# Attention's head pairs traced with the second head first, in scores and in value blocks

## The chip, the core and the metric

The kernel runs on one core of one Trainium2 chip. The metric is the device time of one execution in microseconds (us). Its engines are TensorE (PE; its weight loads are listed as PEld), VectorE (DVE), ScalarE (ACT), GpSimd (POOL) and SyncE (SP).

## What is computed

Four transformer layers over 512 tokens of width 1024, all in float32: two of a first kind, then two of a second. Every layer is a mixer and a feed-forward network, each between two RMS norms. Half of each mixer is an attention of 8 heads of 64 columns; this is the part that the change touches.

```python
# first kind: dilated windows; the three branches are merged by their log-denominators
for window, dilation in ((128, 1), (512, 4), (2048, 16)):
    o, lse = dilated_branch(q, k, v, window, dilation)
attn = sum(softmax(lses)[..., None] * outs)          # the other half: a gated delta rule
# second kind: every query attends to the keys that an indexer's top-k selects
logits = einsum('bqhd,bsd->bqhs', iq, ik) * 64 ** -0.5
score = einsum('bqh,bqhs->bqs', iw, relu(logits))
top_val, top_idx = top_k(where(allowed, score, -inf), 128)
p = softmax(where(valid, einsum('bqhd,bqkhd->bqhk', q, k[top_idx]) * 64 ** -0.5, -inf))
out = einsum('bqhk,bqkhd->bqhd', p, v[top_idx])      # the other half: pooled means
```

## The kernel before

Tokens lie in four tiles of 128. A dense product is three TensorE matmuls on rounded parts (`mm3`, L289 to L291, two high-by-low terms beside the high-by-high one), with weights split by ACT (L267) and DVE (L269, or POOL).

Attention (`attention`) works on units (i, h): query tile i, head h, 32 units a layer, in order of i. It never gathers keys: scores over the first (i + 1) * 128 keys are masked. Two heads that follow each other form a pair, e = 0 and e = 1. The two share the array: a head's 64 columns of q and k lie in rows 0 to 63 (e = 0) or 64 to 127 (e = 1), and its result lies in the same half of the accumulator. A unit goes through these steps:

- scores on PE into a PSUM buffer: one float32 matmul in the first kind (L783 in `plain_scores`), three rounded ones in the second (L794 in `split_scores`, which the second kind's indexer calls too);
- mask and row minimum on DVE (L827), exponent and row sum on ACT (L829), reciprocal of a pair's sums on DVE (L837), scaling on ACT (L838). In the pair DVE and ACT take e = 0 first;
- transposes on PE, i + 1 of them (L845), into a PSUM buffer; a copy back to SBUF (`tb`, two buffers), by ACT for e = 0 (L851) and by DVE for e = 1 (L849), so that e = 1 is the one whose copy is made last;
- products with the values on PE (`pv2`, L864): for each key block j one matmul of e = 0 and one of e = 1, into the two halves of one accumulator `ax`.

The rows of a unit lie in `xc` (first kind) or `qs` (second kind) for e = 0, and in `ta` for e = 1. Scores and transposes share four PSUM buffers named `mm`. The pair's products are traced some five units behind its scores. In the program listing a float32 matmul is one row; in the trace it is two instructions, so that a pair of blocks is x2 in the listing and x4 in the trace.

Attention runs beside other work that generators weave in: dense products at first, then what is left of the delta rule (L1381, first kind) or of the indexer's top-k (`select`, L1686 and L1687 on DVE, sixteen rounds a tile) and of the pooled half (L1718 to L1740, second kind). The queues' orders aren't written by hand. When the program is built, a scheduler keeps a clock of its own and gives each engine, of what it then holds ready, what was traced first. On the chip each engine takes its instructions in that order and waits for semaphores.

Of the kernel before, what the change touches and what calls it, by code (L numbers as in the profile page):

```python
# [91 lines left out]
class Net:  # L92
# [683 lines left out]
    def plain_scores(self, qT, kT):  # L776


        def scores(ss, i, pr):
            w = (i + 1) * P  # L780
            for e, s in enumerate(ss):
                r = self.head_rows(e)
                self.nc.tensor.matmul(s[:, :w], qT[r, pr, i * P:(i + 1) * P], kT[r, pr, :w], start=True, stop=True)  # L783
        return scores

    def split_scores(self, Q, K):


        def scores(ss, i, pr):
            w, c, k = max(2, i + 1) * P, slice(i * P, (i + 1) * P), K(pr)  # L790
            for n, (a, b) in enumerate(((0, 0), (0, 1), (1, 0))):
                for e, s in enumerate(ss):
                    r = self.head_rows(e)
                    self.nc.tensor.matmul(s[:, :w], Q[a][r, pr, c], k[b][r, :w], start=n == 0, stop=n == 2)  # L794
        return scores
# [8 lines left out]
    def attention(self, pool, scores, v, nmask, k0, first, n_first, buf, free, masked=lambda i: True):  # L804

        nc, V, T = self.nc, self.nc.vector, self.nc.tensor
        units = [(i, h) for i in range(NT) for h in range(8)]
        st, acc, sums, late = {}, {}, {}, []  # L810
        depth = 5
        pair = lambda n: n - n % 2

        def qk2(n):
            i, h = units[n]
            ss = [first() if n < n_first else self.mm() for _ in range(2)]
            scores(ss, i, h // 2)
            sums[n] = self.sm.tile([P, 2], F32, name="asum", bufs=6)
            for e, s in enumerate(ss):
                qk(n + e, s)  # L820

        def qk(n, s):
            i, h = units[n]
            w = (i + 1) * P
            pb = buf(n)
            m = self.sm.tile([P, 1], F32, name="amin", bufs=6)
            V.tensor_tensor_reduce(pb[:, :w], s[:, :w], nmask(i), scale=1.0, scalar=FMAX,  # L827
                                   op0=OP.add, op1=OP.min, accum_out=m)
            nc.scalar.activation(pb[:, :w], pb[:, :w], AF.Exp, bias=m, scale=-1.0,  # L829
                                 accum_out=sums[pair(n)][:, n % 2:n % 2 + 1])  # L830
            st[n] = pb

        def norm(n):

            w, s = (units[n][0] + 1) * P, sums[pair(n)]
            if n % 2 == 0:
                V.reciprocal(s, s)  # L837
            nc.scalar.activation(st[n][:, :w], st[n][:, :w], AF.Copy, scale=s[:, n % 2:n % 2 + 1])  # L838

        def tr(n):  # L840
            i, h = units[n]
            pb = st[n]
            pt = self.mm()
            for j in range(i + 1):
                T.transpose(pt[:, j * P:(j + 1) * P], pb[:, j * P:(j + 1) * P], self.ident)  # L845
            w = (i + 1) * P
            pT = pool.tile([P, S], F32, name="tb", bufs=2)
            if n % 2:
                V.tensor_copy(pT[:, :w], pt[:, :w])  # L849
            else:  # L850
                nc.scalar.activation(pT[:, :w], pt[:, :w], AF.Copy)  # L851
            st[n] = pT

        def pv2(n):


            i, h = units[n]
            pT = [st.pop(n + e) for e in range(2)]
            if h == 0:
                acc[i] = self.ax()  # L860
            o = acc[i]
            for j in range(i + 1):
                for e in range(2):
                    T.matmul(o[self.head_rows(e), h // 2 * P:(h // 2 + 1) * P], v[:, j, (h + e) * 64:(h + e + 1) * 64],  # L864
                             pT[e][:, j * P:(j + 1) * P], start=j == 0, stop=j == i, skip_group_check=True)
            if h == 6:
                late.append((i, acc.pop(i)))

        def out(i, o):
            s = slice(i * P, (i + 1) * P)  # L870
            self.split_out(self.four(o), self.hha[:, k0:k0 + 4, s], self.hla[:, k0:k0 + 4, s])

        for n in range(len(units) + depth + 3):
            if n < len(units) and n % 2 == 0:
                while not masked(units[n][0]):
                    yield
                qk2(n)
            if 0 <= n - 3 < len(units):
                norm(n - 3)
            if late and free():  # L880
                out(*late.pop(0))
            if depth < n <= len(units) + depth and (n - depth) % 2 == 0:
                while late and not free():
                    yield
                if late and units[n - depth - 2][1] == 0:
                    out(*late.pop(0))
                pv2(n - depth - 2)
            if 0 <= n - depth < len(units):
                tr(n - depth)
            yield  # L890
        for i, o in late:
            out(i, o)
# [948 lines left out]
```

## Time and profile before

| | us |
|---|---|
| median of three runs | 2632.26 |
| these runs | 2622.97, 2632.26, 2636.4 |
| the profiled execution | 2618.65 |
| its span, first to last instruction | 2616.9 |
| PE busy | 2573.4 |
| DVE busy | 1645.4 |
| ACT busy | 1205.7 |

PE's busy time counts an instruction from its start to its modelled end, and neighbours overlap; where the distance of two starts is meant, the text says so. "Idle before" is time that an engine stood still ahead of an instruction, with the instruction that released it. Each layer has one stretch in which attention runs with little dense work beside it; in the trace these are 252 to 292 us and 955 to 996 us (first kind) and 1558 to 1613 us and 2154 to 2209 us (second kind).

### The profile page before, as it was taken

To read this page: it belongs to the slowest core of one execution; us is meant where nothing else is said; L and a number is where in the kernel's file an instruction comes from. 1 tells how busy PE (TensorE), PEld (TensorE's weight loads), DVE (VectorE), ACT (ScalarE), POOL (GpSimd) and SP (SyncE) were. 2 spreads that over 40 slices of the span, in tenths; PEclk is the share of its full clock that TensorE was granted. 3 is DMA by queue.
4 is the path that set the end of the run, shared out by engine and by line. 5 is a ranking of instruction groups with operands and counts; after the bars stand their busy time and mean duration, and the time that the engine had idled before them with its cause. 6 is when DMAs were issued, how large, how long until landed. Compare 5 with 4: busy or idle time off the path is not lost. (4 is left out here: it accounts for less than half of the span.)

```text
span 2616.9 us, 37121 instructions
## 1 busy us (share of the span) xinstructions
PE 2573.4 (98%) x14376; PEld 2125.0 (81%) x14376; DVE 1645.4 (63%) x3206; ACT 1205.7 (46%) x2032; POOL 266.5 (10%) x356
## 2 busy tenths in 40 slices
PE   8999999999999999999999999999999999999998
PEld 7877788888888868888888766999888776999887
DVE  6946676664487575666726686776325687776434
ACT  5346543343443464433424456466324556456322
POOL 2100110000120001000002331100002330200000
PEclk9999999999999999999999999999999999999999
DMA  5321213333324112223333222232333221322332
GB/s 161 95 86 52 81 41 97 97 97 91 103 70 121 51 33 81 73 92 94 97 93 93 65 73 64 74 97 89 90 96 94 69 73 52 103 81 89 97 90 95
DMA packets 165817, 221.94 MB, mean 85 GB/s; under 512 B 25760, under 2 KB 112520, under 8 KB 165640
## 3 DMA queue, kind: packets, MB, share of 16 engines
q1 hardware_dynamic: 164247, 216.92, 27.6%
q0 software_dynamic: 832, 2.63, 0.4%
q8 instruction: 113, 1.85, 0.3%
q14 instruction: 65, 0.52, 0.1%
q10 hardware_dynamic: 560, 0.01, 0.0%
HBM read 212.70 MB, written 6.83 MB: 84 GB/s over the span
## 5 line engine op out<-in xcount | busy, mean ns | idle before, releaser
L289 PE MATMUL mm<-hh,wh 128*128 128x512 f32 (+2 forms) x1684 | 633.7, 378 | 3.3 <-ACT wh L267 1.1
L269 DVE TENSOR_TENSOR wl<-wr,wh 128x1024 fp32r<-128x1024 f32 (+1 forms) x286 | 353.7, 1237 | 447.5 <-ACT wh L267 443.8
L290 PE MATMUL mm<-hl,wh 128*128 128x512 f32 (+2 forms) x1684 | 633.2, 376 | 0.0
L291 PE MATMUL mm<-hh,wl 128*128 128x512 f32 (+2 forms) x1684 | 627.1, 374 | 0.0
L267 ACT ACTIVATE wh<-wr 128x1024 fp32r<-128x1024 f32 (+1 forms) x310 | 326.4, 1054 | 587.3 <-PE mm L290 242.3
L289 PEld LDWEIGHTS mm<-hh,wh 128*128 128x128 f32 (+1 forms) x1684 | 317.2, 188 | 68.0 <-ACT wh L267 1.5
L291 PEld LDWEIGHTS mm<-hh,wl 128*128 128x128 f32 (+1 forms) x1684 | 315.6, 188 | 62.3 <-DVE wl L269 0.6
L290 PEld LDWEIGHTS mm<-hl,wh 128*128 128x128 f32 (+1 forms) x1684 | 315.9, 188 | 57.4 <-issue 0.3
L289 PE MATMUL mm<-wh,hh 128*128 128x512 f32 x524 | 213.9, 408 | 0.0
L291 PE MATMUL mm<-wh,hl 128*128 128x512 f32 x524 | 207.8, 397 | 0.0
L290 PE MATMUL mm<-wl,hh 128*128 128x512 f32 x524 | 207.8, 396 | 0.0
L289 PEld LDWEIGHTS mm<-wh,hh 128*128 128x128 f32 x524 | 98.7, 188 | 28.3 <-issue 4.9
L291 PEld LDWEIGHTS mm<-wh,hl 128*128 128x128 f32 x524 | 98.7, 188 | 23.6
L290 PEld LDWEIGHTS mm<-wl,hh 128*128 128x128 f32 x524 | 98.9, 189 | 20.9
L1397 DVE TENSOR_TENSOR hl<-hq,hh 128x512 fp32r<-128x512 f32 x92 | 63.1, 688 | 80.7 <-ACT hh L1396 80.5
L1510 ACT ACTIVATE fy<-fxc,par 128x512 f32<-128x512 f32 x88 | 67.1, 810 | 78.4 <-DVE fxc L1507 78.4
L1396 ACT ACTIVATE hh<-hq 128x512 fp32r<-128x512 f32 x92 | 57.2, 622 | 97.6 <-PE dx L290 78.8
L609 ACT ACTIVATE hh<-x,par 128x256 fp32r<-128x256 f32 x128 | 60.9, 504 | 72.6 <-DVE x L690 72.6
L1507 DVE TENSOR_TENSOR fxc<-mm,rrep 128x512 f32<-128x512 f32 x88 | 60.0, 690 | 29.7 <-PE mm L291 25.4
L864 PE MATMUL ax<-tb,v 128*64 128x128 f32 x640 | 68.9, 286 | 7.8 <-DVE tb L849 7.4
L864 PEld LDWEIGHTS ax<-tb,v 128*64 128x64 f32 x640 | 42.8, 136 | 41.4 <-DVE tb L849 16.9
L269 POOL TENSOR_TENSOR wl<-wr,wh 128x1024 fp32r<-128x1024 f32 x24 | 58.4, 2432 | 111.4 <-ACT wh L267 111.2
(793 smaller groups left out, 5389.8 us busy)
## 6 DMA issues: line engine op xcount, KB each, us to landing
wr<-in_w_ff_dram SPq DMA_DIRECT2D x100, 512.0 KB, 3.7
wr<-in_w_in_dram SPq DMA_DIRECT2D x96, 512.0 KB, 3.7
wr<-in_ffn_w_in_dram SPq DMA_DIRECT2D x176, 256.0 KB, 3.2
wr<-in_ffn_w_out_dram SPq DMA_DIRECT2D x44, 512.0 KB, 3.6
wr<-in_w_out_dram SPq DMA_DIRECT2D x32, 512.0 KB, 3.6
tail<-in_w_ff_dram SPq DMA_DIRECT2D x28, 512.0 KB, 4.4
xt<-in_x_dram SPq DMA_DIRECT2D x4, 512.0 KB, 7.5
scm<-dM SPq DMA_DIRECT2D x2, 1024.0 KB, 4.5
```

The lines of the kernel that those rows point to most:

```text
L267: nc.scalar.activation(h[:, :n], r[:, :n], AF.Copy)
L269: eng.tensor_tensor(lo[:, :n], r[:, :n], h[:, :n].bitcast(F32), op=OP.subtract)
L289: t.matmul(out, ah, bh, start=first, stop=False, skip_group_check=shared)
L290: t.matmul(out, ah, bl, start=False, stop=False, skip_group_check=shared)
L291: t.matmul(out, al, bh, start=False, stop=last, skip_group_check=shared)
L609: nc.scalar.activation(self.hh[k][:, c], self.x[k][:, c], AF.Copy, scale=g)
L864: T.matmul(o[self.head_rows(e), h // 2 * P:(h // 2 + 1) * P], v[:, j, (h + e) * 64:(h + e + 1) * 64], pT[e][:, j * P:(j + 1) * P], start=j ...
L1396: nc.scalar.activation(h, hid[k], AF.Copy)
L1397: V.tensor_tensor(lo, hid[k], h.bitcast(F32), op=OP.subtract)
L1507: V.tensor_tensor(xc[:, 2:], pt, rrep, op=OP.mult)
L1510: nc.scalar.activation(y, xc[:, 2:], AF.Identity, scale=w(2), bias=self.pcol("ffn_conv_b", l, r))
```

## The change

In three loops the second head of a pair is now traced ahead of the first: both kinds of scores, and the products with the values. Nothing else is edited; no tile, wait or instruction is added or taken away.

```diff
         def scores(ss, i, pr):
             w = (i + 1) * P
-            for e, s in enumerate(ss):
+            for e, s in reversed(list(enumerate(ss))):
                 r = self.head_rows(e)
                 self.nc.tensor.matmul(s[:, :w], qT[r, pr, i * P:(i + 1) * P], kT[r, pr, :w], start=True, stop=True)
...
             for n, (a, b) in enumerate(((0, 0), (0, 1), (1, 0))):
-                for e, s in enumerate(ss):
+                for e, s in reversed(list(enumerate(ss))):
                     r = self.head_rows(e)
                     self.nc.tensor.matmul(s[:, :w], Q[a][r, pr, c], k[b][r, :w], start=n == 0, stop=n == 2)
...
             for j in range(i + 1):
-                for e in range(2):
+                for e in (1, 0):
                     T.matmul(o[self.head_rows(e), h // 2 * P:(h // 2 + 1) * P], v[:, j, (h + e) * 64:(h + e + 1) * 64],
                              pT[e][:, j * P:(j + 1) * P], start=j == 0, stop=j == i, skip_group_check=True)
```

What the scheduler makes of it: in the program before, the products of the 64 pairs stand on PE in 100 runs of L864 rows; 36 pairs are split, the first block of e = 0 alone and the rest some instructions later (8 in each layer of the first kind, 10 in each of the second). Now they stand in 64 runs, one for each pair, e = 1 ahead of e = 0. DVE and ACT change the order of some instructions around them, POOL and SP change nothing, so all transfers stand as before.

On PE, in the first layer at tile i = 1 and 2 (the trace's 259.7 to 264.4 us); x1 of L864 is one float32 matmul:

```order
 L783 MATMUL mm<-kT,qT 128x384 x2
-L864 MATMUL ax<-tb,v 64x128 x3
+L864 MATMUL ax<-tb,v 64x128 x4
 L845 MATMUL mm<-cst,ta 128x128 x2
 L845 MATMUL mm<-cst,xc 128x128 x3
-L864 MATMUL ax<-tb,v 64x128
-L783 MATMUL mm<-kT,qT 128x384
-L864 MATMUL ax<-tb,v 64x128 x3
-L783 MATMUL mm<-kT,qT 128x384
+L783 MATMUL mm<-kT,qT 128x384 x2
+L864 MATMUL ax<-tb,v 64x128 x4
```

The single block and the rest of its pair have become one run, and the two scores that stood on either side of that rest stand together ahead of it.

On PE, in the third layer at tile i = 3 (the trace's 1593.7 to 1595.3 us), with the tiles' numbers: mm_14015 holds the scores of e = 0, mm_14016 those of e = 1:

```order
+L794 MATMUL mm_14016<-kT_12618,qT_12620 128x512
+L794 MATMUL mm_14016<-w3_12619,qT_12620 128x512
+L794 MATMUL mm_14016<-kT_12618,w2_12621 128x512
 L794 MATMUL mm_14015<-kT_12618,qT_12620 128x512
 L794 MATMUL mm_14015<-w3_12619,qT_12620 128x512
 L794 MATMUL mm_14015<-kT_12618,w2_12621 128x512
-L794 MATMUL mm_14016<-kT_12618,qT_12620 128x512
-L794 MATMUL mm_14016<-w3_12619,qT_12620 128x512
-L794 MATMUL mm_14016<-kT_12618,w2_12621 128x512
```

Such a pair stays one head after the other; only which head comes first is turned round. In each layer of the second kind five pairs of scores stand so in the changed program, and in each of the first kind two pairs stand with other work between the heads.

On DVE, in the third layer at the same place, before:

```order
L837 RECIPROCAL asum<-asum 128x2
L827 ISA qs,amin<-mm,nm_12617 128x512
L827 ISA amin 128x1
L827 ISA ta,amin<-mm,nm_12617 128x512
L827 ISA amin 128x1
L849 COPY tb<-mm 128x384
L837 RECIPROCAL asum<-asum 128x2
L269 TENSOR_TENSOR wl<-wr,wh 128x1024
```

and now:

```order
L837 RECIPROCAL asum<-asum 128x2
L269 TENSOR_TENSOR wl<-wr,wh 128x1024
L827 ISA qs,amin<-mm,nm_12617 128x512
L827 ISA amin 128x1
L827 ISA ta,amin<-mm,nm_12617 128x512
L827 ISA amin 128x1
L849 COPY tb<-mm 128x384
```

The split of a weight tile for the next product stands ahead of the pair's masks instead of behind the copy; the masks still take `qs` (e = 0) ahead of `ta` (e = 1).

## Rows read from the trace of the kernel before

**Rows 1.** The page: span; engines' busy us (share); a group's busy us, mean ns | idle before.

```profile
span 2616.9 us, 37121 instructions
PE 2573.4 (98%) x14376; PEld 2125.0 (81%) x14376; DVE 1645.4 (63%) x3206; ACT 1205.7 (46%) x2032; POOL 266.5 (10%) x356
...
L269 DVE TENSOR_TENSOR wl<-wr,wh 128x1024 fp32r<-128x1024 f32 (+1 forms) x286 | 353.7, 1237 | 447.5 <-ACT wh L267 443.8
```

**Rows 2.** Timeline of PE, first layer: start, duration, instructions, idle before and its releaser.

```profile
252.68 0.66 PE L864 MATMUL ax<-tb,v 128*64 128x128 f32 x8
...
258.56 0.44 PE L845 MATMUL mm<-cst,ta 128*128 128x128 f32 x2
258.93 0.43 PE L864 MATMUL ax<-tb,v 128*64 128x128 f32 x2
259.29 0.44 PE L845 MATMUL mm<-cst,xc 128*128 128x128 f32 x2
259.66 0.94 PE L783 MATMUL mm<-kT,qT 64*128 64x384 f32 x4
260.53 0.65 PE L864 MATMUL ax<-tb,v 128*64 128x128 f32 x6
261.11 0.44 PE L845 MATMUL mm<-cst,ta 128*128 128x128 f32 x2
261.39 0.49 PE L845 MATMUL mm<-cst,xc 128*128 128x128 f32 x3
...
262.17 0.91 PE L783 MATMUL mm<-kT,qT 64*128 64x384 f32 x2
...
263.59 0.91 PE L783 MATMUL mm<-kT,qT 64*128 64x384 f32 x2
...
283.42 1.09 PE L864 MATMUL ax<-tb,v 128*64 128x128 f32 x14 [0.17 <-DVE tb L849]
...
285.78 1.21 PE L864 MATMUL ax<-tb,v 128*64 128x128 f32 x16
```

**Rows 3.** The same timeline, where PE waits behind a single block.

```profile
256.01 0.91 PE L783 MATMUL mm<-kT,qT 64*128 64x384 f32 x2
257.14 0.91 PE L783 MATMUL mm<-kT,qT 64*128 64x384 f32 x2 [0.21 <-DVE amin L827]
...
270.34 0.55 PE L845 MATMUL mm<-cst,xc 128*128 128x128 f32 x3 [0.31 <-ACT xc L838]
...
274.57 1.73 PE L783 MATMUL mm<-kT,qT 64*128 64x512 f32 x4
```

**Rows 4.** Stretches: us; busy time (instructions) of PE, PEld, DVE, ACT, POOL; granted clock; DMA.

```profile
252.00:294.00 42.00, 41.21 (x278) 25.05 (x277) 32.23 (x108) 32.77 (x72) 0.82 (x2) 1.00 0.05 17
1558.00:1613.00 55.00, 51.33 (x327) 32.15 (x327) 44.90 (x124) 39.20 (x92) 8.79 (x12) 1.00 0.08 22
1575.30:1597.80 22.50, 19.86 (x121) 11.79 (x121) 22.34 (x65) 15.74 (x40) 0.84 (x1) 1.00 0.00 1
```

**Rows 5.** Chain of work that ended last, 1556 to 1592 us, shares by line.

```profile
by line: POOL pu L1722 23.1%; DVE sc L1687 22.7%; DVE m L1686 19.0%; DVE ta L827 5.7%; DVE qs L827 5.7%; DVE tb L849 5.5%; DVE hl L1740 5.5%; DVE pu L1718 3.4%; DVE pu L1732 3.2%; DVE hl L896 1.6%; issue 1.6%; DVE asum L837 1.5%; DVE t L173
```

**Rows 6.** The same chain from 1590 us on: start, time, what.

```profile
1596.86 0.43 PE mm L794
1597.28 0.80 PE ax L864 x10
1598.08 0.68 PE mm L794 x4
...
1599.93 0.36 PE ax L864 x2
...
1611.32 0.36 PE ax L864 x2
```

**Rows 7.** Timeline of DVE, first layer, at a pair of scores with products between.

```profile
279.47 0.69 DVE L827 CUSTOM_DVE_ANT_0 xc<-mm,cst 128x512 f32<-128x512 f32 x1 [0.63 <-PE mm L783]
...
281.32 0.69 DVE L827 CUSTOM_DVE_ANT_0 ta<-mm,cst 128x512 f32<-128x512 f32 x1 [0.47 <-PE mm L783]
```

## The prediction

> **What bounds the kernel now.** I read the page first: PE is busy 98% of the span, no other engine over 63% [rows 1]. So time is saved only where PE does the same work in fewer nanoseconds, and only if nothing else holds PE up there. The granted clock is 1.00, the upper level of 2.4 GHz, in all stretches that the change touches [rows 4], before and after the waits in them, so the clock is not at issue. Next I looked at stretches. In the first layer's attention tail PE is busy 41.2 of 42.0 us, DVE 32.2 and ACT 32.8: PE is nearly full, with some waits. In the third layer's tail PE is busy 51.3 of 55.0 and DVE 44.9; within it, from 1575.3 to 1597.8, DVE is busy 22.34 of 22.50 us [rows 4]. The second and fourth layers repeat the first and third. The chain of waits says the same of the second kind: from 1556 us to 1592 its steps are POOL's and DVE's, the top-k above all (L1686, L1687), and PE has no line in it [rows 5]. From about 1592 on PE comes back into the chain [rows 6]. So a nanosecond saved on PE counts in the first kind's tails and in the last 20 us of the second kind's, and not in the 36 us before these.
>
> **The price of a split pair.** The PE timeline prices it [rows 2]. The single block of e = 0 is x2. It starts at 258.93 and the next instruction starts at 259.29: 0.36 us. The transposes ahead of it start at 258.56, 0.37 before it; where no single stands between, transposes follow transposes after 0.28 (261.11 to 261.39). So a single adds 0.36 + 0.09 = 0.45. What does the pair save when it is whole? The rest without the single (x6) lasts 0.65, a whole pair of two key blocks (x8) 0.66, because the two heads work in different halves of the array at once; with four key blocks the rest (x14) lasts 1.09 and the whole (x16) 1.21. So mending a split saves 0.44 at one or two key blocks, 0.45 - 0.12 = 0.33 at four; for three no whole pair is shown and I take the middle, 0.38, with the other two as its ends.
>
> Splits in a layer of the first kind are 3 with two blocks, 4 with three and 1 with four: 1.32 + 1.52 + 0.33 = 3.2 us. In a layer of the second kind there is 1 with one block, 4 with two, 3 with three and 2 with four: 2.20 + 1.14 + 0.66 = 4.0 us. One pair of scores in each layer of the first kind is mended too: the two heads alone last 0.91 and 0.91, together 0.94 [rows 2], so up to 0.88 more. Over four layers: 2 x (3.2 + 0.9 + 4.0) = 16.2 us of PE time. That is the upper end.
>
> **What of it is given back.** A whole pair starts when e = 1's copy is there. Where PE would wait for that, or for the next thing behind it, the single had filled a gap and its removal buys nothing.
>
> First kind. Three of the eight singles stand ahead of a wait [rows 3]. Behind the one ahead of 256.01 the second score stands still until DVE has freed a buffer (257.14, idle 0.21, and 1.13 us after the first one's start); ahead of 270.34 PE is idle 0.31 for ACT's scaled row; behind the one ahead of 274.57 the two scores last 1.73, since the second waits for its buffer. I take 0.44 + 0.38 + 0.38 = 1.2 off. The mended score needs both buffers at once, and in the same stretch a buffer came late by as much as the wait at 257.14, so I take half of its 0.88. That leaves 3.2 - 1.2 + 0.4 = 2.4 us a layer. Bounds: 0 if every whole pair waits, 4.1 if none does.
>
> Second kind. Six of the ten splits lie between 1556 and 1592 us, where the chain has nothing of PE [rows 5]: one of one block, four of two, one of three, 2.20 + 0.38 = 2.6 us that becomes waiting of PE. Of the four behind, two are steps of the chain, at 1599.93 and 1611.32, each 0.36 long [rows 6]; with three and four blocks they give 0.38 + 0.33 = 0.7. The other two are covered by ACT and DVE. There is one more gain: at 1596.86 one score matmul, then the products (0.80), then the other scores (0.68) stand ahead of DVE's minimum [rows 6], 1.91 us; now the products come last, and the scores run one head after the other. How long this takes is bounded by 0.43 + 0.68 = 1.1 below and 1.9 above (as before); near the upper end, since a head alone loses the overlap: 0.2 us. Sum 0.9 us a layer, bounds 0 and 1.4 + 0.8.
>
> DVE's weight split, moved ahead of a pair's masks, is the same instruction. In the program before, it stood behind the copy; now it delays the masks only if DVE isn't waiting for the scores there, and turning the heads round makes it wait (next part). I cost it at nothing; if that cover is gone it costs its own length, 1.24 us [rows 1], in each of the two layers. Transfers don't move, as SP and POOL have the same instructions in the same order.
>
> Sum: 2 x 2.4 + 2 x 0.9 = 6.6 us. On the profiled execution (2618.65) this gives 2612.0. That execution lies 13.6 below the median, inside the spread of runs (2622.97 to 2636.4) or just under it, so I carry the difference over to the median: 2632.26 - 6.6 = 2625.7 us, a quarter of a per cent.
>
> **The rivals.**
>
> *All of it arrives.* The waits of rows 3 shrink as well, because products and scores that come earlier on PE start DVE and ACT earlier. For: in the first kind DVE itself stands still for scores of PE (0.63 and 0.47 us, [rows 7]), so a faster PE feeds it. Against: 36 us of the second kind's tail hang on DVE and POOL alone. The time: 2632.3 - 16.2 = 2616.1.
>
> *Nothing arrives.* The single of e = 0 was ready work put into time in which PE would have waited for e = 1's copy. Now e = 0 stands behind e = 1 on PE, and if PE waits at each whole pair until the moment at which the rest started before, the 0.65 of the rest becomes the 0.66 of the whole and no more. For: at rows 3's 270.34 PE does stand still for one instruction with others queued behind it. Against: the timeline shows 0.17 to 0.31 us of idle time at such places [rows 2, 3], less than the 0.45 of a single, and none around 258.93. The time: 2632.3, unchanged. The Trainium skill has a rule for this, in "TensorE: Matmul & The Clock Gate", Part 3 on row and column tiling: matmuls start and end in program order, and only weight loads are pulled ahead. By that rule a ready block behind a late one can't pass it, which speaks against the change; the idle 0.31 us at 270.34 agrees. That the order does not change as announced is no separate case: all 36 splits are gone from the listing.
>
> *Slower: scores now end in the wrong order.* DVE still takes e = 0's minimum first, and now e = 0's scores come last. Where both run at once that costs nearly nothing. In pairs that still stand apart (two in each layer of the first kind, five in each of the second), DVE holds a finished e = 1 and waits for e = 0. Price: before, it did e = 0's 0.69 us while PE was at e = 1 [rows 7]; now both follow the later score, so 0.69 us a pair. It decides where DVE has nothing else and its result is waited for at once. In all 14 pairs that would be 9.7 us, 2642; outside the 36 us that hang on DVE anyway it would be two pairs a layer in both kinds, eight in all, 5.5 us, and if the singles give nothing, the time is 2637.8. Against: at 1596.86 the products no longer stand between a pair's scores, so that one ends earlier whichever head is last.
>
> **How the numbers follow.** Chances: the forecast (3 to 10 us faster) 0.60; all of it 0.15; nothing 0.17; slower 0.08. About 0.5%, 13 us, is what a measurement of this kernel can tell from no change. Faster by over that needs nearly the whole 16.2 us: most of the second case and a small part of the first, 0.15. Slower by over 13 us is beyond the worst price above and is left with 0.03, for a wait that I don't see. Within: 0.82. The range goes from 2612 (all of it, and a median some 4 us lucky) to 2639 (the slower case); the runs of before lie 13 us apart, and this more than the change sets its width.
>
> **What would show it right or wrong.** In the profile after: L864 on PE in 64 runs (x4, x8, x12, x16) and no x2 outside the one-block pairs; x12 between the 0.66 of x8 and the 1.21 of x16; transposes of `xc` some 0.28 behind those of `ta`. In the first kind's tails two to three us less from the first whole pair to the dense product behind; waits of PE for DVE's copy at L864 longer than the 0.17 at 283.42 [rows 2]. In the second kind's tails the top-k ends when it did, PE idles more before 1592, and the gain appears behind it. DVE's idle time ahead of L827 at the pairs that stay apart, above the 0.6 of rows 7, would show the slower case. I am wrong if the tails shrink by over 5 us each (waits fall too), if they don't shrink (all was cover), or if time moves in stretches where the listing shows no change.

## The result

In the first comparison the changed kernel took 2612.72 us (median of 7 runs, 2610.84 to 2619.66) beside 2631.78 for the kernel before (7 runs, 2622.97 to 2638.13). The ratio is 0.9944, 95% interval 0.9927 to 0.9962: 0.56% faster, where the forecast was 0.25% (2625.7 us). (This ratio and those below are the comparisons' own estimates and not quotients of the medians; that quotient would be 0.9928 here.) A second comparison, with 12 runs of it and 35 of before, gave 2616.21 beside 2626.18, ratio 0.9969 (0.9956 to 0.9982). So it is faster, by 10 to 19 us of median, and the forecast of 6.6 us was too small. The 19 are in part chance: in four later comparisons the kernel before has medians of 2624.04 to 2626.18, and not 2631.78. Yet the two profiled executions lie 6.85 us apart (2618.65 and 2611.80), almost the forecast. Both facts have to be explained, and the second turned out to be partly luck: in the one profile the clock did not fall in the second kind's tails, in the other it did.

### The profile page after: what moved, and what is told of

It reads as the page before. It is cut to its first block, busy times and chain, and to the rows that moved or that the text cites. A ratio compares the mean times of both kernels' runs of the same rounds, so it can differ in the third digit from the quotient of the medians.

```text
span 2610.0 us, 37091 instructions
## 1 busy us (share of the span) xinstructions
PE 2558.5 (98%) x14376; PEld 2119.5 (81%) x14376; DVE 1644.3 (63%) x3206; ACT 1204.5 (46%) x2032; POOL 266.4 (10%) x356
## 5 line engine op out<-in xcount | busy, mean ns | idle before, releaser
L289 PE MATMUL mm<-hh,wh 128*128 128x512 f32 (+2 forms) x1684 | 633.9, 379 | 3.1 <-ACT wh L267 1.1
L269 DVE TENSOR_TENSOR wl<-wr,wh 128x1024 fp32r<-128x1024 f32 (+1 forms) x286 | 353.3, 1235 | 444.9 <-ACT wh L267 441.0
L291 PE MATMUL mm<-hh,wl 128*128 128x512 f32 (+2 forms) x1684 | 626.7, 373 | 0.0
L289 PEld LDWEIGHTS mm<-hh,wh 128*128 128x128 f32 (+1 forms) x1684 | 317.0, 188 | 67.6 <-ACT wh L267 1.5
L291 PEld LDWEIGHTS mm<-hh,wl 128*128 128x128 f32 (+1 forms) x1684 | 315.9, 188 | 62.1 <-DVE wl L269 0.3
L289 PE MATMUL mm<-wh,hh 128*128 128x512 f32 x524 | 213.9, 408 | 0.0
L291 PE MATMUL mm<-wh,hl 128*128 128x512 f32 x524 | 207.9, 397 | 0.0
L289 PEld LDWEIGHTS mm<-wh,hh 128*128 128x128 f32 x524 | 98.6, 188 | 28.2 <-issue 4.9
L291 PEld LDWEIGHTS mm<-wh,hl 128*128 128x128 f32 x524 | 98.7, 188 | 23.6
L269 POOL TENSOR_TENSOR wl<-wr,wh 128x1024 fp32r<-128x1024 f32 x24 | 58.3, 2429 | 111.4 <-ACT wh L267 111.1
L289 PE MATMUL ax<-hh,wh 128*128 128x512 f32 (+1 forms) x186 | 66.4, 357 | 0.0
L290 PE MATMUL ax<-hl,wh 128*128 128x512 f32 (+1 forms) x186 | 66.3, 357 | 0.0
```

Source lines behind the costliest of these rows:

```text
L269: eng.tensor_tensor(lo[:, :n], r[:, :n], h[:, :n].bitcast(F32), op=OP.subtract)
L289: t.matmul(out, ah, bh, start=first, stop=False, skip_group_check=shared)
L290: t.matmul(out, ah, bl, start=False, stop=False, skip_group_check=shared)
L291: t.matmul(out, al, bh, start=False, stop=last, skip_group_check=shared)
```

## The profile after

The page of the changed kernel, span and busy us (share) of the engines, against [rows 1]:

```profile
span 2610.0 us, 37091 instructions
PE 2558.5 (98%) x14376; PEld 2119.5 (81%) x14376; DVE 1644.3 (63%) x3206; ACT 1204.5 (46%) x2032; POOL 266.4 (10%) x356
```

PE's busy time fell by 14.9 us (2573.4 before), near the 16.2 of the upper end. The span fell by 6.9. So most of the PE work went, and half of that came back as time in which PE stands still.

The timeline of PE in the first layer of the changed kernel (start, duration, instructions, idle before and releaser), against [rows 2, 3]:

```profile
257.14 0.91 PE L783 MATMUL mm<-kT,qT 64*128 64x384 f32 x2 [0.42 <-DVE amin L827]
...
259.12 0.66 PE L864 MATMUL ax<-tb,v 128*64 128x128 f32 x8
...
268.21 0.88 PE L864 MATMUL ax<-tb,v 128*64 128x128 f32 x12
...
270.31 0.55 PE L845 MATMUL mm<-cst,xc 128*128 128x128 f32 x3 [0.75 <-ACT xc L838]
...
276.14 0.88 PE L864 MATMUL ax<-tb,v 128*64 128x128 f32 x12 [0.39 <-DVE tb L849]
...
283.50 1.09 PE L864 MATMUL ax<-tb,v 128*64 128x128 f32 x16 [0.77 <-DVE tb L849]
285.42 1.09 PE L864 MATMUL ax<-tb,v 128*64 128x128 f32 x16
```

The singles are gone and the pairs are whole: x8 in 0.66, x12 in 0.88, x16 in 1.09. The transpose of `xc` at 270.34 in [rows 3] is the one at 270.31 here. (That the two times are near each other means nothing: this tail starts 1.14 us later in its execution, at 250.23 and not 249.09, as the windows below show.) The single that stood ahead of it is gone, and the wait for ACT's scaled row has grown from 0.31 to 0.75, by the 0.44 that a single costs: here the saving was given back whole, as predicted for this place. New are the waits of whole pairs for DVE's copy (0.39, 0.77), where [rows 2] had 0.17.

To say what each tail gained, take four stretches, each from the start of a dense matmul (L289 to L291) ahead of a tail to the start of another behind it, the same two matmuls in every kernel. Windows of the kernel before over these stretches (us; PE's busy time and instructions, granted clock, DMA share, GB/s):

```profile
249.09:300.01 50.92, 50.13 (x316) 1.00 0.10 32
940.01:1005.22 65.21, 64.43 (x391) 1.00 0.14 44
1545.26:1640.04 94.78, 90.08 (x530) 1.00 0.23 68
2140.07:2240.09 100.02, 94.88 (x565) 1.00 0.24 70
```

and of the changed kernel:

```profile
250.23:299.40 49.17, 46.19 (x316) 1.00 0.10 34
938.80:1002.24 63.44, 60.47 (x390) 1.00 0.14 44
1542.23:1635.69 93.46, 85.67 (x529) 0.96 0.23 68
2133.91:2233.19 99.28, 91.97 (x566) 0.95 0.24 70
```

First kind: 1.75 and 1.77 us shorter. PE is busy 3.94 us less in the first (forecast: up to 4.1), and idle 2.98 where it was 0.79. Second kind: 1.32 and 0.74 shorter (forecast 0.9 each). Sum 5.6; the other 1.3 lies outside these stretches, in places where two executions of the kernel before also differ, by 1 to 5 us each. And the last column but two holds what the prediction had ruled out: in the second kind's tails the granted clock is no longer 1.00.

## The experiments

All comparisons, each with the kernel before run beside it:

| | median us | before us | ratio, 95% interval |
|---|---|---|---|
| before again | 2628.40 | 2626.18 | 1.0004 (0.9988 to 1.0019) |
| after again | 2616.21 | 2626.18 | 0.9969 (0.9956 to 0.9982) |
| products only | 2623.98 | 2626.18 | 0.9989 (0.9976 to 1.0001) |
| scores only | 2621.49 | 2626.18 | 0.9994 (0.9976 to 1.0011) |
| first kind only | 2626.77 | 2624.04 | 0.9996 (0.9978 to 1.0014) |
| second kind only | 2616.56 | 2624.04 | 0.9962 (0.9945 to 0.9979) |
| before, half top-k | 2604.17 | 2624.04 | 0.9915 (0.9892 to 0.9939) |
| after, half top-k | 2593.93 | 2624.04 | 0.9873 (0.9851 to 0.9896) |
| products only, half top-k | 2596.82 | 2625.46 | 0.9882 (0.9860 to 0.9904) |
| before, filler | 2631.00 | 2625.18 | 1.0020 (1.0006 to 1.0034) |
| after, filler | 2628.48 | 2625.18 | 1.0008 (0.9996 to 1.0021) |
| masks in turn | 2622.13 | 2625.18 | 0.9986 (0.9974 to 0.9997) |

### The same two kernels once more

Nothing is edited. 

> The kernel before, once more, to see its granted clock run by run. In the two profiles the changed kernel's span is 6.9 us shorter (2616.9 to 2610.0), but the timed runs stand some 15 us apart. Theory A (the order of PE's work alone): all runs of before cost the same but for chance, their mean clock is about the 0.998 of its profile, and times from 2623 to 2638 have another cause. Theory B (the clock): the timed runs of before spend more time at the half clock than its profile did; mean clock 0.990 to 0.995, and about 2.6 us for each 0.001 below 0.998, so 2625 to 2638 us.

> The changed kernel beside the same runs. Theory A: 6 to 8 us below before at equal clock. Theory B: clock 0.993 to 0.996 and 2610 to 2619 us; the gap to before falls to about 7 us where two executions of equal mean clock are compared, and is 12 to 19 us between the medians.

The 35 runs of before in this comparison spread from 2617.9 us, at a mean granted clock of 0.998, to 2638.8 at 0.988: some 2 us for each 0.001, so the spread goes with the clock, as theory B has it. The gap between the kernels follows neither theory: at an equal mean clock of 0.994 five runs of the changed kernel took 2615.0 to 2617.0 us and eight of the kernel before 2626.2 to 2628.5, some 11 us apart and not the 6 to 8 that both expect there. A mean clock doesn't tell where the clock fell. The two profiles show where the clock fell. Windows of before again, second kind's stretches as above, then around the fall:

```profile
1551.67:1651.11 99.44, 95.15 (x529) 0.93 0.22 65
2150.04:2251.11 101.07, 96.00 (x566) 0.98 0.23 69
...
1570.00:1597.90 27.90, 25.68 (x146) 1.00 0.06 19
1597.90:1611.60 13.70, 13.12 (x54) 0.50 0.14 40
```

and of after again:

```profile
1544.61:1638.79 94.18, 87.03 (x529) 0.95 0.23 68
2136.98:2236.53 99.55, 91.89 (x565) 0.95 0.23 70
...
1560.00:1579.10 19.10, 16.34 (x96) 1.00 0.10 28
```

A granted clock of 0.50 is the lower level, 1.2 GHz. In both kernels PE had stood still several times just before (busy 25.68 of 27.90 and 16.34 of 19.10 us). In the kernel before this stretch at half clock lies behind 1590 us and the tail is 4.66 us longer than in its first profile (99.44 against 94.78). In the changed one it lies ahead of 1590, and the tail is only 0.72 longer than in its own first profile. That one had half clock at the same place, for 6.8 us, so 0.72 is what 3.4 us more of it cost; no tail of the changed kernel at full clock is on record to set either against.

The last step of the top-k, which writes the mask (L1690), splits such a tail in two. In the third layer it stands here, in this order: before, before again, after, after again.

```profile
1592.28 0.41 DVE L1690 TENSOR_SCALAR nm<-sc 128x512 f32<-128x512 f32 x1
1598.69 0.41 DVE L1690 TENSOR_SCALAR nm<-sc 128x512 f32<-128x512 f32 x1
1588.98 0.41 DVE L1690 TENSOR_SCALAR nm<-sc 128x512 f32<-128x512 f32 x1
1592.07 0.42 DVE L1690 TENSOR_SCALAR nm<-sc 128x512 f32<-128x512 f32 x1
```

From the tail's start to this step it is 47.02 and 47.02 us in the kernel before, 46.75 and 47.46 in the changed one. Behind it 47.76 and 52.42 us are left in the one, 46.71 and 46.72 in the other. In the fourth layer 51.71 and 52.76 are left in the one and 50.69 twice in the other, and where the clock stays at 1.00 behind the step the profiles of one kind alone, further down, repeat these lengths to 0.03 (47.77, 46.73, 50.70). So what the order gains in every execution, 1.0 us a layer, lies behind the top-k's last step. There the kernel before also pays for its half clock, and the changed one had none there.

Why the place matters is in the chain of waits (the work that ended last, shares by line). Over the half-clock stretch of before again, 1597.9 to 1611.6:

```profile
by line: PE mm L794 33.5%; PE ax L864 31.0%; PE mm L845 28.8%; DVE sc L1687 4.8%; DVE tb L849 3.4%; DVE asum L837 0.5%; issue 0.3%
```

and over that of the first profile of the changed kernel, 1578.8 to 1585.6:

```profile
by line: DVE sc L1687 39.0%; DVE m L1686 26.6%; DVE hl L1740 9.7%; DVE hl L896 8.7%; DVE ta L827 7.9%; DVE qs L827 6.7%; issue 4.8%; DVE tb L849 4.7%; DVE amin L827 1.4%; DVE asum L837 0.9%
```

In the one the chain is PE's, so slow matmuls count. In the other it is DVE's. DVE's busy time says the same; windows of all engines (PE, PEld, DVE, ACT, POOL) over the half clock, of after and of after again:

```profile
1578.80:1585.60 6.80, 6.24 (x27) 3.71 (x25) 6.80 (x20) 5.20 (x14) 0.00 (x0) 0.50 0.00 0
1579.10:1589.30 10.20, 9.53 (x41) 5.54 (x39) 9.78 (x29) 6.46 (x17) 0.00 (x0) 0.50 0.00 0
```

DVE never stands still in the first and 0.42 us in the second, so the slow matmuls are hidden there, wholly or nearly. So the order of the change was not the whole of it: the clock explains the spread within a kernel, and part of the gap between kernels.

### Products only, scores only

```diff
-                for e in range(2):
+                for e in (1, 0):
```

for the products (L864) alone, and for the scores alone, in both functions:

```diff
-            for e, s in enumerate(ss):
+            for e, s in reversed(list(enumerate(ss))):
```

> Only the products with the values (L864) are traced with the second head first; both scores stay as before. If the 36 split pairs carry the gain, as the prediction's sum has it (14.4 of 16.2 us of PE time), nearly all of it is here: 64 runs of L864 and a ratio within 0.001 of the changed kernel's. If the scores' order carries it, the ratio is near 1.000.

> Only the two kinds of scores are traced with the second head first; the products stay as before. The prediction's sum gives them one mended pair in each layer of the first kind (0.4 to 0.9 us a layer) and, as the slower rival, up to 0.69 us for each pair that stays apart: between 2 us faster and 6 us slower, ratio 0.999 to 1.002. If the scores carry the gain: 0.995.

By medians the parts give 2.2 and 4.7 us, the whole 10; the interval of neither part leaves out 1.000, so the runs alone don't show that either part is faster. The stretches say why the medians don't add up. Windows of products only:

```profile
254.41:304.07 49.66, 47.02 (x316) 1.00 0.10 33
...
1548.40:1644.88 96.48, 88.39 (x530) 0.93 0.22 66
2143.46:2244.43 100.97, 91.92 (x565) 0.95 0.22 69
```

and of scores only:

```profile
250.49:300.13 49.64, 47.89 (x316) 1.00 0.10 34
...
1543.08:1645.12 102.04, 97.69 (x529) 0.90 0.21 63
2143.24:2242.51 99.27, 93.98 (x565) 1.00 0.25 74
```

In the first kind, at a clock of 1.00 throughout, each part takes 1.3 us off (50.92 to 49.66 and to 49.64) and both together 1.75: they overlap. Scores alone leave all 36 singles; what they mend is two pairs of scores a layer (L783 stands in 36 runs, 40 before), each worth up to 0.88. In the second kind the clock decides more than the part: the longest tail here, 102.04, belongs to the kernel that gained 0.75 in the other layer, at full clock.

### One kind of layer at a time

The whole change, made to depend on the kind of layer (`k0 == 0` in the products is the first kind; `plain_scores` is the first kind's, `split_scores` the second's):

```diff
-                for e in (1, 0):
+                for e in ((1, 0) if k0 == 0 else (0, 1)):
```

> The whole change (scores and products turned round), in the two layers of the first kind only; the second kind is as before. Both theories give the same here: the first kind's two tails shrink by 1.8 us each, as they did in the profile after (starts of the same PE instructions at 250 and 294 us, and at 950 and 1000 us, set against each other), and the second kind's tails keep the times of before, at equal granted clock. Sum -3.5 us. If the second kind's tails move by more than 1 us at a granted clock of 1.00, something outside the touched rows carries time and both fall.

> The whole change in the two layers of the second kind only. Theory A (the prediction: DVE's top-k hides most of it, 0.9 us a layer): -1.8 us, 0.999 of before. Theory C (nearly all of the 4.0 us a layer arrives when both kernels run at the same granted clock, and stretches at half clock in these tails take part of it back): -6 to -8 us at a mean granted clock equal to that of before, and less in proportion as the mean clock is lower, by some 2 us for each 0.001.

Windows of first kind only:

```profile
253.63:302.80 49.17, 46.19 (x316) 1.00 0.11 33
...
1550.38:1645.15 94.77, 90.10 (x529) 1.00 0.23 68
2143.89:2252.71 108.82, 104.78 (x566) 0.89 0.23 66
```

and of second kind only:

```profile
1545.33:1638.80 93.47, 85.81 (x529) 0.96 0.22 68
2137.04:2235.74 98.70, 90.50 (x566) 0.97 0.25 71
```

The first kind's tail has the same 49.17 as with the whole change: the 1.75 is real. But the median does not show it (2626.77 beside 2624.04, inconclusive), since the untouched second kind scatters by more: 94.77, the length of before to 0.01, in one layer, and 108.82 at a clock of 0.89, 8.8 us too long, in the other (the profiled execution, 2632.03 us, is the slowest of its 12). Second kind only is 7.5 us faster by median, far more than the 1.3 a layer by which its tails are shorter than those of before at full clock.

Six tails of either order close the gap. With the old order (before, before again, first kind only) they took 94.78, 99.44 and 94.77 in the third layer and 100.02, 101.07 and 108.82 in the fourth, on average 96.33 and 103.30. With the new one (after, after again, second kind only): 93.46, 94.18, 93.47 and 99.28, 99.55, 98.70, on average 93.70 and 99.18. That is 2.6 + 4.1 = 6.8 us, and with the first kind's 3.5 it makes 10.3. Measured were 7.5 (second kind alone) and 10.0 (all). With six tails of each, one of them out of the slowest run of its kernel, this is an agreement, not a proof.

### Half of the top-k

Eight instead of sixteen rounds of top-k, so half of the selection is left out. It takes half of L1686 and L1687 off DVE, and with them much of what the prediction held to be the bound of these tails.

```diff
-            for it in range(16):
+            for it in range(8):
```

> The kernel before with 8 instead of 16 rounds of top-k in the second kind: half of the selection is left out, so half the time of L1686 and L1687 is gone from DVE. It is the base for the next run. If PE's waits for DVE are what the clock falls on, the second kind's tails show no stretch at half clock, and are shorter than before by several us. If the clock falls for a reason that has nothing to do with these waits, stretches of 3 to 14 us at half clock stay there.

> The changed kernel with 8 instead of 16 rounds of top-k, to be set against the run before it. With DVE's chain gone from the second kind's tails, Theory A gives the full PE saving there, 4.0 us a layer where the changed kernel gave 0.9: with the first kind's 3.5 a gap of 11 to 12 us to the run before. If DVE's chain is not what held the gain back, the gap stays what it is without the cut: 7 us between undisturbed executions, 10 between medians. Theory C expects no large change of the gap at equal clock (10 to 12 us), but that both kernels lose their stretches at half clock in the tails.

> Only the products turned round (L864 in 64 runs, scores as before), with 8 instead of 16 rounds of top-k, so half of the selection is left out: to be set against the two earlier runs with 8 rounds, whose second-kind tails have no half clock. If the whole pairs of products are what saves time, as the prediction's price has it, the first kind's tails shrink by 1.3 us each (as they did with products alone before) and the second kind's by 3.5 to 4.0 us each, 10 us in all against the kernel before with 8 rounds. If the turned scores carry a part of it, the second kind's tails shrink by 2 us or less each, 6 us in all.

Windows of before with half the top-k:

```profile
1543.96:1632.03 88.07, 87.01 (x529) 1.00 0.25 73
2130.43:2223.00 92.57, 91.51 (x565) 1.00 0.27 79
```

of the whole change with it:

```profile
1549.47:1633.47 84.00, 82.22 (x529) 1.00 0.26 76
2131.93:2220.46 88.53, 86.75 (x566) 1.00 0.27 78
```

and of the products alone with it:

```profile
249.06:298.71 49.65, 47.01 (x316) 1.00 0.11 33
...
1541.34:1625.33 83.99, 82.27 (x529) 1.00 0.24 76
2124.21:2212.74 88.53, 86.82 (x565) 1.00 0.26 78
```

With PE idle only 1.1 to 1.8 us, the clock stays at 1.00 in all six tails. And the change now gives 4.07 and 4.04 us a tail, where it gave 1.32 and 0.74. The four tails make 11.6 us, which both theories allow (11 to 12 and 10 to 12). Halving the top-k took DVE's load and the half clock away at once, so by itself it doesn't say which of the two had swallowed the rest. DVE's waits do. In the kernel before, from the third layer's tail's start to the top-k's last step (us in total, times, longest), then the windows of all engines over this stretch, of before and of the changed kernel:

```profile
DVE t L1730 <- POOL pu L1722: 3.0, 2, 2.1
DVE tb L849 <- PE mm L845: 0.4, 1, 0.4
...
1545.26:1592.28 47.02, 42.98 (x228) 26.48 (x226) 43.27 (x125) 27.63 (x76) 12.90 (x18) 1.00 0.11 34
...
1542.23:1588.98 46.75, 40.41 (x226) 25.21 (x224) 43.16 (x125) 27.50 (x76) 12.89 (x18) 0.93 0.11 35
```

DVE is busy 43.27 of the 47.02 us, stands 3.0 for POOL, and for PE only 0.4, all at a clock of 1.00. So a faster PE had little to give there, and half clock took little from the changed kernel's 46.75: it was DVE's own work, the top-k above all, that held the saving back, as theory A said. The gap of medians is 10.2 (2604.17 and 2593.93), the mean granted clock of the changed kernel's runs being 0.001 lower. Products alone give 4.08 and 4.04, so with half the top-k the turned scores carry nothing in the second kind; in the first kind they carry 0.5 of the 1.75.

The price of a single is confirmed as well. With half the top-k the scheduler splits 11 pairs in each layer of the second kind; PE is busy 4.79 us less when they are whole, 0.44 each.

### Filler for PE's waits

The first score product of the second kind's attention is computed twice, with the first result overwritten.

```diff
-            for n, (a, b) in enumerate(((0, 0), (0, 1), (1, 0))):
+            for n, a, b in ((-1, 0, 0),) * twice + ((0, 0, 0), (1, 0, 1), (2, 1, 0)):
```

> The kernel before, with the first of the three score products of the second kind's attention computed twice: 32 more matmuls (16 pairs) in each layer of the second kind, about 0.12 to 0.24 us a pair, so 2.6 us of PE work a layer; nothing else changes. Theory D (PE's waits for DVE in the second kind's tails are what the clock falls on, and where it falls behind 1590 us it costs 0.3 to 0.4 us for each us at half clock): the waits are partly filled, so half clock in these tails becomes rarer, the times lie closer together than the 2618 to 2639 of before, and their median is no higher than that of before in spite of 5 us more work. Rival (the clock falls whatever PE does there): the spread stays and the median rises by 1.5 to 5 us.

> The changed kernel with the same 32 doubled matmuls in each layer of the second kind, against the run before it. Theory D: with the clock at 1.00 in both, the gap is the order's alone, 3.5 us of the first kind and 1 to 4 of the second (1.2 a layer if DVE's chain still ends last, up to 4.0 if the filler makes PE the last): 6 to 11 us. If half clock stays in the tails of the changed kernel alone, the gap is smaller than 6.

Their tails stand in the table of the last section. Both expectations of theory D failed. The times of before with filler still spread (2625.0 to 2634.9) and their median rose by 5.8 us; the gap to the changed kernel is 2.5 us, not 6 to 11. The busy times show that the filler did not fill the waits, it lengthened them. PE is idle 5.2 and 6.2 us (4.7 and 5.1 without filler), and in the changed kernel 10.2 and 9.6. The doubled product stands ahead of the scores that DVE waits for, which would make DVE's copies later too; this is a reading of the order, not a run's result. As a test of what holds the clock up it is void.

### DVE and ACT in turn

In the changed kernel the masks and exponents also take e = 1 first:

```diff
-            for e, s in enumerate(ss):
+            for e, s in reversed(list(enumerate(ss))):
                 qk(n + e, s)
```

> The changed kernel with the masks and minima on DVE, and so the exponents on ACT, also taken with e = 1 first, in the order in which the scores now end. The prediction (at most pairs both scores run together, so DVE's order costs nothing): within 1 us of the changed kernel at equal granted clock, and DVE's idle time ahead of the first minimum of a pair as in the changed kernel. The slower rival of the prediction (DVE waits for the later score at pairs that stand apart, 0.69 us each at up to eight pairs that count): 3 to 5.5 us faster than the changed kernel.

Its window in the first layer (the second kind's stand in the table of the last section):

```profile
253.49:303.13 49.64, 47.01 (x315) 1.00 0.10 34
```

Neither expectation holds: it is not faster but slower than the changed kernel, by 0.47 us in the first layer's tail and by about 2 in the second kind's, where the time at half clock differs too. All three lengths are those of products alone to within 0.8 us (49.66, 96.48, 100.97). In both of these kernels scores and masks take the two heads in the same order. What the turned scores gain, they gain only against a DVE that keeps the old order; why, I can't show.

## Why the prediction came out as it did

**The bound.** Right for the second kind, but for the scores (below): the part of its tails ahead of 1592 us hung on DVE and POOL [rows 4, 5], and halving the top-k freed the hidden saving. Forecast 0.9 us a layer, measured 1.32 and 0.74 from profile to profile. Of these 1.05 and 1.02 lie behind the top-k's last step, where the forecast put them, and the rest ahead of it: 0.27 won in the third layer, 0.28 lost in the fourth, both at some half clock.

**"The clock is not at issue" failed.** [Rows 4] show 1.00, but of one execution. That profile (2618.65) was one in which the second kind's tails never fell to half clock; in the two other profiles with the old order there they did in three tails of four, at up to 8.8 us. So the step that failed with it is the carrying over: "that execution lies 13.6 below the median, so I carry the difference over". The 13.6 us were not luck to be added to both kernels. A good part of them was half clock in PE's chain, behind the top-k's last step; in the changed kernel's profiles it lies ahead of that step, where DVE is nearly always busy. By the tails' averages this makes up the 3 to 4 us beyond the forecast in the second comparison. For the 19 us of the first comparison I can't show it, as the clocks of before's runs aren't known there.

**The price of a split.** 0.44 for one and two key blocks was right. For three and four it was too small: x12 takes 0.88 against 0.87 of the rest (0.87, x10, at 268.29 in before), x16 1.09 against 1.09 of x14. The 1.21 of [rows 2] was no odd row: the ten whole pairs of four blocks in the kernel before took 1.18 to 1.24, one of them

```profile
290.33 1.24 PE L864 MATMUL ax<-tb,v 128*64 128x128 f32 x16
```

and all sixteen of the changed one 1.09 or 1.10. In the first layer's three the first block of e = 1 starts 0.09 to 0.16 us behind that of e = 0, where 0.01 is usual, so the old order had a short wait inside the whole pair as well. So 0.44 in place of the guessed 0.38 and of 0.33, and some 0.1 us at whole pairs of four blocks, which the sum put at nothing. One sign failed: the transposes of `xc` follow those of `ta` after 0.28 us at 256.34, but after 0.53 at 260.24 and 262.80. PE's busy time fell by 14.9 us, in spite of some stretches at half clock, against an upper end of 16.2.

**What is given back, first kind.** Mis-sized: 1.2 us for the singles and 0.44 for the scores, where PE's idle time rose by 2.19 (0.79 to 2.98). Two of the three places I named behaved as said (257.14 and 270.34); what I had not counted are the whole pairs at 276.14 and 283.50, which wait 0.39 and 0.77 for e = 1's copy. Hence 1.75 and not 2.4.

**The score term, second kind.** I had 0.2 us for a pair whose scores no longer have products between them. With the top-k halved, turned scores changed the second kind's tails by 0.01 us or less. In the kernel as it is, scores alone took 0.75 off the fourth layer's tail at full clock, 0.65 of it ahead of the top-k's last step (47.66 us behind the tail's start, against 48.31); in the third layer the step came 0.61 earlier (46.41, against 47.02). So the gain lies where the prediction let nothing on PE count, and not where it had put the 0.2. These are two layers of one execution.

**The weight split of L269**, costed at nothing: in the changed kernel it runs from 1591.26 for 1.20 us and the mask behind it starts at 1592.38, 0.33 after its scores' end (1592.05). So the cover held but for a third of a microsecond.

**The rivals.** *All arrives* is refuted for the kernel as it is, and is what happens in the second kind with half the top-k (4.07 a tail). *Nothing arrives* is right in single places: at 270.31 the saving turned into a wait with other matmuls queued behind it, but over the tail 1.75 of 3.94 us stays. That fits the rule of the Trainium skill that matmuls run in program order ("TensorE: Matmul & The Clock Gate", Part 3). *Slower* did not come: DVE's wait for scores grew at one pair (1.43 us at 280.88, where [rows 7] have 0.63 and 0.47), 0.33 at that pair and not 0.69, while over the whole first tail its waits for scores fell from 2.0 to 1.4 us, and turning DVE's order round too made things worse.

**The range** held the time 0.7 us above its low end, and its width, taken from the spread of before, was what made it hold. That is partly luck: the forecast's own 3 to 10 us were passed in the first comparison (19) and just met in the second (10.0).

## What to carry to other kernels

Take a profile more than once before ruling the clock out: a stretch in which PE waits for another engine can run at either level from one execution to the next, and the median of many runs holds both. Price a change at the same pair of instructions ahead of and behind a stretch (here they repeat to 0.03 us where the clock is 1.00), and let medians only say whether it sums up. To learn whether an engine hides a saving, halve that engine's work and see whether the saving appears in full; look at the granted clock too, since here the halving changed both, and at what that engine waited for before.

## What the runs showed of the hardware

Second kind's tails, with PE's idle time (length less busy) and the granted clock, from windows as above:

| | third layer: us, idle, clock | fourth layer: us, idle, clock |
|---|---|---|
| before, half top-k | 88.07, 1.06, 1.00 | 92.57, 1.06, 1.00 |
| after, half top-k | 84.00, 1.78, 1.00 | 88.53, 1.78, 1.00 |
| products only, half top-k | 83.99, 1.72, 1.00 | 88.53, 1.71, 1.00 |
| before | 94.78, 4.70, 1.00 | 100.02, 5.14, 1.00 |
| before again | 99.44, 4.29, 0.93 | 101.07, 5.07, 0.98 |
| first kind only | 94.77, 4.67, 1.00 | 108.82, 4.04, 0.89 |
| scores only | 102.04, 4.35, 0.90 | 99.27, 5.29, 1.00 |
| before, filler | 97.09, 5.22, 0.98 | 104.70, 6.22, 0.97 |
| after | 93.46, 7.79, 0.96 | 99.28, 7.31, 0.95 |
| after again | 94.18, 7.15, 0.95 | 99.55, 7.66, 0.95 |
| second kind only | 93.47, 7.66, 0.96 | 98.70, 8.20, 0.97 |
| products only | 96.48, 8.09, 0.93 | 100.97, 9.05, 0.95 |
| masks in turn | 95.69, 8.51, 0.95 | 100.91, 9.98, 0.97 |
| after, filler | 99.52, 10.15, 0.97 | 105.13, 9.60, 0.95 |

The six tails with half the top-k kept a clock of 1.00. Of the ten with the old order of the products and the whole top-k it fell in six, and in all twelve with the new order. Behind the top-k's last step, in PE's own chain, a fall cost 0.31 to 0.37 us for each us at half clock (1.05 us for 3.4, 4.66 for 13.7, 8.8 for 23.9). Ahead of it, in DVE's chain, 10.2 us in place of 6.8 put that step 0.6 to 0.9 us later in the tails of the changed order. That PE's waits cause the falls is what the halved top-k speaks for, and no run shows it: since a slower clock also changes the waits, and the first kind's tails stand 3 us idle at 1.00, the table is no rule. What decides between executions of one program, and the falls outside of the tails (at 140, 736 and 841 us in several profiles of either kernel), stays open.
